# SyncE's transfers of the two down stages of a hybrid decoder layer, chained to each other in program order

## Chip, core and metric

The kernel runs on one core of a Trainium2 chip. The metric is the device time of one execution in microseconds (us); less is better. The core has a matrix engine (PE, with its weight loads as PEld), a vector engine (DVE), a scalar engine (ACT), GpSimd (POOL) and SyncE (SP), which does no arithmetic and issues most of the DMA transfers. Each engine takes its instructions in the order in which the program has them. An instruction whose data are not there holds up all that stand behind it on the same engine, on SP too.

## The reference, cut to what matters

One decoder layer for 2048 tokens and a model width of 1024: three token mixers, an output projection, and a squared-ReLU MLP whose second product is the "down" stage of this case.

```python
    x = x + jnp.einsum("bsc,cd->bsd", mix, w_out)
    h2 = rmsnorm(x, norm2_g)
    ff = jnp.square(jax.nn.relu(jnp.einsum("bsd,df->bsf", h2, w_up)))
    return x + jnp.einsum("bsf,fd->bsd", ff, w_down)   # then a final rmsnorm
```

ff is 2048 x 4096 and w_down 4096 x 1024, all in float32.

## The kernel before

The tokens are worked on in two halves of 1024 (`h` = 0 and 1). For each half come an output projection (`outproj`), an up stage (`up`) and a down stage (`down`); the down stage of half 0 begins at about 968 us of the trace, that of half 1 at 1712 us. Every float32 operand is split by `halves` into a rounded part and a remainder: ACT makes the rounded part (L891), DVE the remainder (L892), and PE multiplies in three passes (L1423 to L1425).

A down stage is a two by two block product in seven products instead of eight (`PRODUCTS` = 1, 2, 7, 6, 4, 5, 3, the order of n = 0 to 6). Each product is eight steps, so a half has 56 steps, g = 0 to 55, of 24 matmuls. One step needs two operands:

- the moving operand, written by the up stage to the DRAM scratch `fscr` and loaded by `s_load` (L1266, 512 KB) into one of six pairs of tiles. `S_AT` names them: in the program's names the pairs are `rounded_73`, `rounded_74`, `rounded_77` twice and `rounded_78` twice, in turn. `s_split` halves it in place. This is what the change's short name calls the first operand of a step;
- the weight block, loaded by `t_load` from w_down: for n = 0 straight into its tile (L1282), later into `kept` (eight blocks, one for each kp = g mod 8) and `second` (a ring of three) (both L1279, 512 KB each). `t_sum` adds or subtracts the two on DVE (L1292, L1294, L1296, result in `kept`), and `t_split` halves the sum into one of six weight pairs. Products 7 and 5 load both blocks for each step, 2 `kept` only, 6, 4 and 3 `second` only.

`ahead(g)` says which of these is asked for at step g: loads up to step g+5, sums up to g+3, splits up to g+2. A pair of the moving operand is free for step g+6 when PE has finished step g. A `kept` block is free when its split is done, a `second` block when its sum is.

The program text is not the order on the engines. A scheduler places each engine's instructions when their operands and tiles are free in its own account; only an explicit dependence added by `tc.add_manual_dep` ties two of them. The output projection already ties its SP instructions in this way (`in_order`); the down stages do not.

At the end of each product (kp = 7) the four PSUM banks are taken out by `evac`: ACT copies for products 1 and 7 (L1429, L1431), DVE additions for product 6 (L1433) and for 2, 4, 5 and 3 (L1436). The first matmul of the next product needs the bank that it writes to be taken out. `res_load` (L1358, 1 MB) and `res_scale` (L1361) bring in the residual. In half 0 the recurrent mixer of half 1 is woven into the down stage by `tick` (L540 to L576, its matmuls L552 to L554); half 1 has nothing woven in.

Of the kernel before, what the change touches and what calls it, by code (L numbers as in the profile page):

```python
# [77 lines left out]
def body(tc, xt, w_in, w_v, w_out, w_up, w_down, vecs, lru_wa, lru_wx, consts, out):  # L78
    nc = tc.nc
# [68 lines left out]
    def conv_bank():  # L148
        return pc.tile([P, NB], F32, name="cb", tag="cb")
# [43 lines left out]
    def v(name, i=0, n=1):  # L193
        at = VEC[name][0] + i
        return vec[:, at:at + n]
# [746 lines left out]
    def out_second(h, pairs):  # L942
        out_load(2, pairs)
        out_load(3, pairs)
        act_load(h, 0, 0, 2)
# [10 lines left out]
    class Weights:  # L956
# [3 lines left out]
        def load(self, f):  # L960
            at = self.at
            nc.sync.dma_start(at[2], w_up[f][:, 2 * NB:3 * NB])
            nc.sync.dma_start(at[0], w_up[f][:, 0:NB])
            nc.sync.dma_start(at[4 + f % 2 * 2], w_up[f][:, NB:2 * NB])
# [25 lines left out]
        def of(self, i, f):  # L990
# [2 lines left out]
            n, c = {1: (0, 0), 6: (0, 1), 7: (2, 0), 5: (2, 1)}.get(i, (4, (i + f + 1) % 2))  # L993
            return [self.pairs[n + j][:, c * NB:(c + 1) * NB] for j in range(2)]

    def outproj(h, wts, banks, begun):
        at, pairs = wts.at, wts.pairs
        s_at = ring(at[0:4])
# [12 lines left out]
        def residual(n):  # L1011
            m, d, tok = where(n)
            nc.sync.dma_start(e_at[n % es], xt[d][:, tok])
# [29 lines left out]

        if not begun:
            out_second(h, pairs)
        queued, mark = [], [len(nc.cur_bb.bb.instructions)]

        def in_order():
            for i in nc.cur_bb.bb.instructions[mark[0]:]:
                if i.engine == mybir.EngineType.SP:  # L1050
                    if queued:
                        tc.add_manual_dep(i, queued[-1].name, mybir.DependencyInfo(
                            mybir.DependencyClass.NoSync, mybir.DependencyReason.DATA), reason="queue")
                    queued.append(i)
            mark[0] = len(nc.cur_bb.bb.instructions)

        residual(0)
        residual(1)
        for n in range(16):
# [274 lines left out]
    def down(h, steps, banks, hooks):  # L1334
# [13 lines left out]
        def part(t, j):  # L1348
            return t[:, j * NB:(j + 1) * NB]

        def tok(m):
            return slice(h * HS + m * NB, h * HS + (m + 1) * NB)
# [21 lines left out]
        def finish(m, zs, load=None):  # L1374
            r, t = sq[m], tmps[0]
            for j in range(3):
                q = tmps[j % 2]
                nc.scalar.activation(q, part(zs[-1], j), AF.Square)
                nc.vector.tensor_add(r, r, q)
                if j == 1:  # L1380
                    yield
            q = tmps[1]
            nc.scalar.activation(q, part(zs[-1], 3), AF.Square)
            nc.scalar.activation(t, mrow[:, m * NB:(m + 1) * NB], AF.Square, scale=RMS_EPS ** 0.5)
            yield
            bank = conv_bank()
            nc.tensor.matmul(bank, ones_d, r, start=True, stop=False)
            nc.tensor.matmul(bank, ones_d, q, start=False, stop=True)
            if load is not None:
                load()  # L1390
            yield
            nc.vector.tensor_add(r, t, bank)
            nc.scalar.activation(r, r, AF.Sqrt)
            yield
            nc.vector.reciprocal(r, r)
            yield
            for dh in (1, 0):
                for j in range(4):
                    d = 4 * dh + j
                    y = part(zs[dh], j)  # L1400
                    nc.vector.scalar_tensor_tensor(y, y, v("final_g", d), r, op0=OP.mult, op1=OP.mult)
                    if j % 2:
                        yield
                        for q in (j - 1, j):
                            (nc.sync if h and not m else nc.gpsimd).dma_start(out[4 * dh + q][:, tok(m)], part(zs[dh], q))
# [32 lines left out]
        def aside_of(n, kp):  # L1438
# [16 lines left out]
            elif i == 5:  # L1455
# [8 lines left out]
                elif kp == 6:  # L1464
                    nc.vector.tensor_add(vv, vv, u)

        for g in range(56):
            n, kp = divmod(g, 8)
            i = PRODUCTS[n]
            ahead(g)  # L1470
            aside_of(n, kp)
            edge = kp in (0, 7)
            if n == 6:
                hooks(kp)
            for x in range(8):
                j, kk = divmod(x, 2) if edge else (x % 4, x // 4)
                matmuls(g, j, kk)
                if kp == 7 and kk:
                    with first():
                        evac(i, j)  # L1480
                if x in (3, 7):
                    tick(DOWN_SHARE)
            if kp == 7:
                if i == 6:
                    nc.vector.tensor_add(vv, vv, u)
                elif i == 2:
                    chores.append(squares(0, z0, True))
                    nc.scalar.dma_start(yscr[:, :, tok(0)].rearrange("j p n -> p j n"), three(z0))
                elif i == 4:
                    chores.append(squares(1, z1, True))  # L1490
                elif i == 5:
                    chores.append(finish(1, (z1, z0)))

        def again():
            nc.gpsimd.dma_start(three(z1), yscr[:, :, tok(0)].rearrange("j p n -> p j n"))
# [134 lines left out]
```

## Time and profile before

| what | value |
|---|---|
| runs | 2038.21, 2041.81 and 2046.28 us; median 2041.81 us |
| profiled execution, its own time | 2037.72 us |
| its span, first to last instruction | 2035.9 us |
| PE busy | 1966.7 us, 97% of the span |
| DVE, ACT, POOL busy | 1466.1, 1053.8 and 168.4 us |
| mean granted clock of PE | 0.994 of full speed |
| DMA | 416.32 MB, mean 204 GB/s |

A group of rows in the profile gives a line, an engine, the tiles (out<-in), a count, busy time, and the idle time before it with what ended that. A row of waits says which instruction waited for which, how long in total, how often, and the longest. Line numbers are those of the kernel before.

### The profile page before, as it was taken

How to read it: one execution, taken by the hardware profiler on the slowest of the kernel's cores; microseconds unless marked ns; L12 is line 12 of the kernel's file. 1: busy time of each engine (PE TensorE's matmuls, PEld its weight loads, DVE VectorE, ACT ScalarE, POOL GpSimd, SP SyncE). 2: the span in 40 equal slices, each digit the busy share in tenths (PEclk: the TensorE clock that was granted, in tenths of full speed). 3: DMA queues.
4: the chain of work that ended last, by engine and by line, in shares of the span. 5: the costliest groups of instructions: out<-in, count | busy, mean ns of one | idle time of the engine just before them, and what ended most of it. 6: DMA issues, size and time to landing. Idle time of an engine off the chain costs nothing.

```text
span 2035.9 us, 25608 instructions
## 1 busy us (share of the span) xinstructions
PE 1966.7 (97%) x8876; PEld 1587.4 (78%) x8876; DVE 1466.1 (72%) x1977; ACT 1053.8 (52%) x1623; POOL 168.4 (8%) x296
## 2 busy tenths in 40 slices
PE   7999999999999999999999899989999999999997
PEld 6877777878777777888788778767888888888885
DVE  7899865578677656878889796677555555686854
ACT  6144875333667655465565654356455455444441
POOL 0123100100113413000000000100000000000001
PEclk9999999999999999999999999999999999999998
DMA  5555584843786647445997765685444437997643
GB/s 166 172 149 161 171 290 152 268 130 114 231 274 189 199 148 254 150 166 189 331 337 244 270 199 166 230 276 180 148 151 151 152 140 253 339 330 234 218 145 114
DMA packets 208766, 416.32 MB, mean 204 GB/s; under 512 B 26134, under 2 KB 34566, under 8 KB 208572
## 3 DMA queue, kind: packets, MB, share of 16 engines
q1 hardware_dynamic: 189220, 358.27, 52.7%
q0 software_dynamic: 16208, 45.91, 7.7%
q10 hardware_dynamic: 3208, 10.49, 1.5%
q8 instruction: 70, 1.15, 0.2%
q14 instruction: 60, 0.49, 0.1%
HBM read 299.79 MB, written 123.19 MB: 208 GB/s over the span
## 4 chain that ended last, share of the span: by engine, by line
PE 73%; DMA 11%; DVE 9%; ACT 4%; issue 3%; SPq 1%; DVEq 0%; POOL 0%; ACTq 0%
PE bank L1113 9%; PE bank L1114 9%; PE bank L1115 9%; PE bank L1423 8%; PE bank L1424 8%; PE bank L1425 8%; PE mm L255 4%; PE mm L258 4%; PE mm L261 3%; DMA rounded<-fscr 2%; DMA pair<-out_w 2%; DMA raw<-in_xt 2%; DVE wide L462 1%; DVE rounded L892 1%; PE bank L929 1%
## 5 line engine op out<-in xcount | busy, mean ns | idle before, releaser
L1113 PE MATMUL bank<-rounded,pair 128*128 128x512 f32 x896 | 354.2, 396 | 2.9 <-ACT low L1193 1.6
L1114 PE MATMUL bank<-rounded,pair 128*128 128x512 f32 x896 | 352.7, 394 | 0.0
L1115 PE MATMUL bank<-rounded,pair 128*128 128x512 f32 x896 | 350.8, 391 | 0.0
L891 ACT CAST rounded<-rounded 128x1024 fp32r<-128x1024 f32 (+1 forms) x168 | 160.4, 967 | 277.5 <-DMA rounded<-fscr 220.7
L892 DVE TENSOR_TENSOR rounded<-rounded 128x1024 fp32r<-128x1024 f32 (+1 forms) x168 | 186.0, 1119 | 124.6 <-ACT rounded L891 124.1
L1423 PE MATMUL bank<-rounded,rounded 128*128 128x512 f32 x576 | 225.4, 391 | 8.4 <-DVE u L1433 5.5
L1425 PE MATMUL bank<-rounded,rounded 128*128 128x512 f32 x576 | 224.7, 390 | 0.0
L1424 PE MATMUL bank<-rounded,rounded 128*128 128x512 f32 x576 | 224.7, 390 | 0.0
L1113 PEld LDWEIGHTS bank<-rounded,pair 128*128 128x128 f32 x896 | 168.1, 188 | 43.5 <-issue 2.6
L1115 PEld LDWEIGHTS bank<-rounded,pair 128*128 128x128 f32 x896 | 168.3, 188 | 37.5 <-issue 0.6
L1114 PEld LDWEIGHTS bank<-rounded,pair 128*128 128x128 f32 x896 | 168.3, 188 | 36.0 <-issue 0.7
L255 PE MATMUL mm<-rounded,rounded 128*128 128x512 f32 x496 | 160.7, 399 | 9.3 <-ACT rounded L235 7.5
L261 PE MATMUL mm<-rounded,rounded 128*128 128x512 f32 x496 | 158.8, 395 | 0.0
L258 PE MATMUL mm<-rounded,rounded 128*128 128x512 f32 x496 | 157.9, 395 | 0.0
L235 ACT CAST rounded<-raw 128x512 fp32r<-128x512 f32 (+1 forms) x96 | 55.8, 583 | 157.3 <-PE mm L258 105.1
L1423 PEld LDWEIGHTS bank<-rounded,rounded 128*128 128x128 f32 x576 | 108.5, 188 | 32.9 <-DVE u L1433 6.1
L891 ACT CAST pair<-wraw 128x1024 fp32r<-128x1024 f32 x64 | 67.2, 1051 | 114.3 <-PE bank L1114 112.7
L1423 PE MATMUL bank<-rounded 128*128 128x512 f32 x320 | 125.5, 392 | 0.7 <-ACT v L1431 0.7
L1424 PEld LDWEIGHTS bank<-rounded,rounded 128*128 128x128 f32 x576 | 108.6, 188 | 22.6
L1425 PEld LDWEIGHTS bank<-rounded,rounded 128*128 128x128 f32 x576 | 108.4, 188 | 22.7
L1425 PE MATMUL bank<-rounded 128*128 128x512 f32 x320 | 124.7, 390 | 1.1 <-DVE rounded L892 1.1
L1424 PE MATMUL bank<-rounded 128*128 128x512 f32 x320 | 124.6, 389 | 0.0
(323 smaller groups left out, 3815.1 us busy)
## 6 DMA issues: line engine op xcount, KB each, us to landing
fscr<-low SPq DMA_DIRECT2D x224, 256.0 KB, 2.2
rounded<-fscr SPq DMA_DIRECT2D x112, 512.0 KB, 4.4
second<-in_w_down SPq DMA_DIRECT2D x80, 512.0 KB, 6.0
kept<-in_w_down SPq DMA_DIRECT2D x48, 512.0 KB, 5.7
raw<-in_w_in SPq DMA_DIRECT2D x64, 256.0 KB, 3.9
wraw<-in_w_up SPq DMA_DIRECT2D x64, 256.0 KB, 2.9
low<-in_w_up SPq DMA_DIRECT2D x64, 256.0 KB, 3.3
pair<-out_w SPq DMA_DIRECT2D x24, 512.0 KB, 5.3
```

Of the source, the lines that this page charges most:

```text
L235: nc.scalar.copy(h, raw)
L255: nc.tensor.matmul(bank, wh[:, sl], ah[:, cols], start=first_, stop=False)
L258: nc.tensor.matmul(bank, wh[:, sl], al[:, cols], start=False, stop=False)
L261: nc.tensor.matmul(bank, wl[:, sl], ah[:, cols], start=False, stop=last_)
L891: nc.scalar.copy(h, raw)
L892: nc.vector.tensor_sub(l, raw, f32(h))
L1113: nc.tensor.matmul(bank, wh[:, sl], hi(x), start=fresh and k == 0, stop=False, **kw)
L1114: nc.tensor.matmul(bank, wh[:, sl], lo(x), start=False, stop=False, **kw)
L1115: nc.tensor.matmul(bank, wl[:, sl], hi(x), start=False, stop=k == KH - 1, **kw)
L1423: nc.tensor.matmul(banks[j], th[:, c], sh[:, x], start=fresh and k0, stop=False, **kw)
L1424: nc.tensor.matmul(banks[j], th[:, c], sl[:, x], start=False, stop=False, **kw)
L1425: nc.tensor.matmul(banks[j], tl[:, c], sh[:, x], start=False, stop=k1, **kw)
```

## The change

The helper that ties SP's instructions to each other in the order in which they were traced moves out of `outproj` into a function of its own, `sp_order`. `outproj` calls it and is as it was. `down` calls it too: once ahead of the 56 steps, and `in_order()` at the end of each step. So every SP instruction traced during a down stage is tied to the one traced before it. The dependence is one of order only: it puts no semaphore on the chip.

```diff
+    def sp_order():
+        queued, mark = [], [len(nc.cur_bb.bb.instructions)]
+
+        def in_order():
+            for i in nc.cur_bb.bb.instructions[mark[0]:]:
+                if i.engine == mybir.EngineType.SP:
+                    if queued:
+                        tc.add_manual_dep(i, queued[-1].name, mybir.DependencyInfo(
+                            mybir.DependencyClass.NoSync, mybir.DependencyReason.DATA), reason="queue")
+                    queued.append(i)
+            mark[0] = len(nc.cur_bb.bb.instructions)
+
+        return in_order
+
     def outproj(h, wts, banks, begun):
...
-        queued, mark = [], [len(nc.cur_bb.bb.instructions)]
-
-        def in_order():
...
+        in_order = sp_order()
         residual(0)
...
+        in_order = sp_order()
         for g in range(56):
             n, kp = divmod(g, 8)
             i = PRODUCTS[n]
...
                 elif i == 5:
                     chores.append(finish(1, (z1, z0)))
+            in_order()
```

The traced order of a step is the one of `ahead`: first the moving operand of step g+5, then the weight block or blocks of step g+5, then a residual load where there is one. PE's and POOL's rows stand in the same order before and after. SP's, DVE's and ACT's change inside the two down stages.

On SP before, in half 0, this stands where products 6 and 4 meet. The two rows of `rounded_78` are the moving operands of steps 34 and 35, the `rounded_73` is that of step 36; `kept_7672` to `kept_7675` are blocks of steps 40 to 43:

```order
L1266 DMA rounded_77<-fscr 128x2x512 x2
L1279 DMA kept_7672<-in_w_down 128x2x512
L1279 DMA kept_7673<-in_w_down 128x2x512
L1266 DMA rounded_78<-fscr 128x2x512
L1279 DMA second_7695<-in_w_down 128x2x512
L1279 DMA kept_7674<-in_w_down 128x2x512
L1266 DMA rounded_78<-fscr 128x2x512
L1279 DMA second_7696<-in_w_down 128x2x512
L1279 DMA kept_7675<-in_w_down 128x2x512
L1279 DMA second_7697<-in_w_down 128x2x512
L1266 DMA rounded_73<-fscr 128x2x512
```

On SP after, the same five moving operands (their line is now L1270, the blocks' L1283), each with the one block of its own step:

```order
L1270 DMA rounded_77<-fscr 128x2x512
L1283 DMA second_7697<-in_w_down 128x2x512
L1270 DMA rounded_77<-fscr 128x2x512
L1283 DMA second_7695<-in_w_down 128x2x512
L1270 DMA rounded_78<-fscr 128x2x512
L1283 DMA second_7696<-in_w_down 128x2x512
L1270 DMA rounded_78<-fscr 128x2x512
L1283 DMA second_7697<-in_w_down 128x2x512
L1270 DMA rounded_73<-fscr 128x2x512
```

The blocks of steps 40 to 43 have moved from between the moving operands of steps 33 to 36 to behind those of steps 40 to 43.

On DVE before, at the end of product 6 of half 0 (steps 30 and 31; L892 is a split, L1292 a sum for product 5, L1433 the evacuation):

```order
L892 TENSOR_TENSOR rounded_78<-rounded_78 128x1024
L892 TENSOR_TENSOR rounded_76<-kept_7675,rounded_76 128x1024
L1292 TENSOR_TENSOR kept_7674<-kept_7674,second_7695 128x1024
L892 TENSOR_TENSOR rounded_78<-rounded_78 128x1024
L892 TENSOR_TENSOR rounded_73<-kept_7676,rounded_73 128x1024
L1292 TENSOR_TENSOR kept_7675<-kept_7675,second_7696 128x1024
L1433 TENSOR_TENSOR u<-u,bank_4017 128x512
L1433 TENSOR_TENSOR u<-u,bank_4018 128x512
```

On DVE after, the same place (L1300 is a sum for product 4, L1437 the evacuation):

```order
L892 TENSOR_TENSOR rounded_78<-rounded_78 128x1024
L1300 TENSOR_TENSOR kept_7674<-second_7696,kept_7674 128x1024
L892 TENSOR_TENSOR rounded_76<-kept_7674,rounded_76 128x1024
L892 TENSOR_TENSOR rounded_78<-rounded_78 128x1024
L1300 TENSOR_TENSOR kept_7675<-second_7697,kept_7675 128x1024
L892 TENSOR_TENSOR rounded_76<-kept_7675,rounded_76 128x1024
L1437 TENSOR_TENSOR u<-u,bank_4017 128x512
L1437 TENSOR_TENSOR u<-u,bank_4018 128x512
```

Before, the evacuation of step 31 stands behind the split of step 36's weights and a sum for step 43. After, it stands behind the sum and the split of step 35's weights. In both, the split of step 35's moving operand stands ahead of it.

## Rows read from the trace of the kernel before

**Rows 1.** The page's busy time, share of the span and instructions of each engine.

```profile
PE 1966.7 (97%) x8876; PEld 1587.4 (78%) x8876; DVE 1466.1 (72%) x1977; ACT 1053.8 (52%) x1623; POOL 168.4 (8%) x296
```

**Rows 2.** PE's waits from 967 to 1304 us: total, times, longest.

```profile
PE bank L1423 <- DVE u L1433: 5.5, 1, 5.5
PE bank L1423 <- DVE z L1436: 1.6, 2, 1.3
PE bank L1423 <- ACT u L1429: 1.3, 1, 1.3
PE bank L1425 <- DVE rounded L892: 1.1, 1, 1.1
PE bank L1423 <- ACT v L1431: 0.7, 1, 0.7
PE cb L276 <- DVE mr L236: 0.7, 1, 0.7
```

**Rows 3.** PE's waits from 1640 us to the end.

```profile
PE cb L1387 <- DVE sum L1379: 1.4, 1, 1.4
```

**Rows 4.** Stretches of half 0: length, PE, PEld, DVE, ACT, POOL, PEclk, DMA share, GB/s.

```profile
1155.70:1161.30 5.60, 0.15 (x1) 0.00 (x0) 4.47 (x6) 5.16 (x6) 0.00 (x0) 0.99 0.92 308
1161.30:1164.70 3.40, 3.38 (x8) 2.71 (x9) 1.76 (x3) 3.14 (x5) 0.00 (x0) 0.52 0.87 313
1164.70:1170.10 5.40, 5.40 (x25) 4.28 (x25) 5.01 (x5) 3.56 (x5) 0.00 (x0) 1.00 0.87 300
```

**Rows 5.** DVE's timeline ahead of the long wait.

```profile
1157.17 1.23 DVE L892 TENSOR_TENSOR rounded<-rounded 128x1024 fp32r<-128x1024 f32 x1 [1.13 <-ACT rounded L891]
1158.31 1.22 DVE L892 TENSOR_TENSOR rounded<-kept,rounded 128x1024 fp32r<-128x1024 f32 x1
1159.45 1.22 DVE L1292 TENSOR_TENSOR kept<-kept,second 128x1024 f32<-128x1024 f32 x1
1160.58 1.28 DVE L1433 TENSOR_TENSOR u<-u,bank 128x512 f32<-128x512 f32 x2
```

**Rows 6.** ACT's timeline there.

```profile
1151.27 1.05 ACT L891 CAST rounded<-rounded 128x1024 fp32r<-128x1024 f32 x1 [11.12 <-DMA rounded<-fscr]
1156.09 1.04 ACT L891 CAST rounded<-rounded 128x1024 fp32r<-128x1024 f32 x1 [2.83 <-DMA rounded<-fscr]
```

**Rows 7.** SP's timeline there (issues only).

```profile
1140.99 1.46 SPq L1279 DMA_DIRECT2D kept<-in_w_down  x2
1142.55 0.63 SPq L1266 DMA_DIRECT2D rounded<-fscr  x1
1143.27 0.77 SPq L1279 DMA_DIRECT2D second<-in_w_down  x1
1149.20 0.37 SPq L1279 DMA_DIRECT2D kept<-in_w_down  x1
1149.66 0.42 SPq L1266 DMA_DIRECT2D rounded<-fscr  x1
```

**Rows 8.** SP's waits from 967 to 1298 us.

```profile
SPq L1266 <- PE bank L1425: 130.2, 35, 7.0
SPq L1279 <- DVE rounded L892: 41.5, 15, 8.1
```

**Rows 9.** SP's timeline in half 1.

```profile
1870.01 0.37 SPq L1266 DMA_DIRECT2D rounded<-fscr  x1
1875.45 0.37 SPq L1266 DMA_DIRECT2D rounded<-fscr  x1
1880.89 0.37 SPq L1266 DMA_DIRECT2D rounded<-fscr  x1
```

**Rows 10.** Landings, min/median/max: all `fscr` operands (L1266), the `second` blocks, the residual loads (L1358).

```profile
DMA to landing us min/median/max: 3.4/4.4/9.2
...
DMA to landing us min/median/max: 3.2/6.0/10.5
...
DMA to landing us min/median/max: 5.1/8.7/9.2
```

**Rows 11.** The second product of half 0 and the fourth of half 1, columns as in rows 4.

```profile
1016.10:1063.10 47.00, 46.71 (x204) 38.21 (x204) 39.75 (x42) 30.92 (x37) 2.14 (x4) 1.00 0.94 333
1842.80:1886.40 43.60, 43.60 (x194) 36.08 (x194) 29.77 (x27) 17.39 (x19) 0.00 (x0) 1.00 0.72 238
```

**Rows 12.** ACT at the end of the first product of half 0.

```profile
1013.62 1.05 ACT L891 CAST rounded<-rounded 128x1024 fp32r<-128x1024 f32 x1 [8.41 <-DMA rounded<-fscr]
1015.52 1.56 ACT L1429 COPY u<-bank 128x512 f32<-128x512 f32 x3
```

More of the change, by code (lines that the diff above doesn't have):

```diff
@@ L1045, in outproj @@
             out_second(h, pairs)
-        queued, mark = [], [len(nc.cur_bb.bb.instructions)]
-        def in_order():
[L1049 to L1055, printed above, removed]
+        in_order = sp_order()
         residual(0)
```

## The prediction

> **What bounds the kernel now.** I read the page's busy times first, then PE's waits by stretch, then, backwards from the longest wait, the timelines of DVE, ACT and SP, and last the landing times. PE is busy for 1966.7 of 2035.9 us [rows 1], so a reordering of transfers can win only what PE loses by waiting inside the two down stages, and can lose anything. In half 0 the waits at the ends of products are 5.5 (product 6, behind the DVE additions of L1433), 1.6 in two (products 2 and 4, L1436), 1.3 (product 1, ACT) and 0.7 us (product 7, ACT): 9.1 us [rows 2]. The other two rows there, 1.1 and 0.7 us, lie in the first steps, where SP's order is not changed. From 1640 us to the end, which holds all of the down stage of half 1, PE waits 1.4 us in all, and that is for the final norm [rows 3]. So half 0 has 9.1 us to give, half 1 nothing.
>
> The long wait has a tail. In the 3.40 us after it PE ran 8 matmuls at a granted clock of 0.52, the lower of its two levels (1.2 GHz), and then 25 in 5.40 us at 1.00 [rows 4]. At the full clock the 8 take 8 x 5.40 / 25 = 1.73 us, so the lower clock cost 3.40 - 1.73 = 1.7 us, behind 5.5 us in which PE had nothing to do. The most that can be won is 9.1 + 1.7 = 10.8 us.
>
> **Where the long wait comes from.** PE stands from 1155.7 to 1161.3 us [rows 4]. The bank that it needs is taken out by the L1433 that begins at 1160.58. DVE was not idle but late: in front stand the split of a moving operand at 1157.17, which had waited for ACT, a weight split and a sum [rows 5]. ACT had waited 2.83 us for the `fscr` transfer that this split reads, and 11.12 us for the one of the step before [rows 6]. That transfer of the step before is step 34's, issued at 1142.55 right behind two `kept` blocks of products to come, and ACT got it only at 1151.27, 8.7 us later, against a median landing of 4.4 [rows 7, 10]. Step 35's was issued at 1149.66, right behind a `kept` block that SP could issue only at 1149.20 [rows 7]; that block is the one of step 42, as the order of before shows, and it waited for a split on DVE to give the block free. So a weight block wanted seven steps later stood in front of an operand that was wanted now. Over this down stage SP waited 41.5 us, in 15 places, for a split to free a block, and 130.2 us, in 35, for PE to free a moving operand [rows 8]. The second kind of wait is the right one: nothing can be loaded sooner. The first is what the chain takes out from in front of it.
>
> **The change, part by part.** (1) No instruction is added or taken out; PE and POOL keep their order; SP issues the same transfers. (2) Moving operands: each now goes out when PE has finished the step that frees its tiles, with nothing ahead of it that waits for anything else. Half 1 shows what this looks like, though its order is the old one: operands leave SP at 1870.01, 1875.45 and 1880.89, one every 5.44 us, which is one step of PE [rows 9], and PE does not wait there [rows 3]. Queued behind such a wait on SP are the blocks of the same step, so they too now go out at the start of a step, five steps before use and not some eleven, as that of step 42 did while PE was in step 31. (3) On DVE the sums for blocks far ahead leave the stretch in front of the evacuations, but the sum and the weight split of step g+4 now stand there, and these need a transfer issued only one step ago.
>
> What (3) may cost must be worked out, end by end. Let T be the start of the last step of product 6, whose end is T + 5.44. Step 35's moving operand is issued at T - 5.44 and its block about 0.4 later (an SP issue took 0.37 to 0.46 [rows 7]). At the median of 6.0 us [rows 10] the block lands at T + 1.0. Then one DVE sum (1.22), ACT's part of the split (1.05), DVE's (1.22) and the first evacuation, half of 1.28 [rows 5, 6], are done at T + 5.1. That is 0.3 us before PE needs the bank. In half 1 the order has an evacuation ahead of that split, so the first bank is free at T + 2.9, 2.5 us early. The same count, with the instructions that stand ahead in the order of after, gives 2.0 us to spare at the end of product 2 (two blocks for each step, a sum, no split) and 1.5 at the end of product 5 (a split, no sum). At the end of product 4 a residual load and its scaling stand ahead; issued two steps before at T - 9.5 and landing in 8.7 us, 9.2 at most [rows 10], it is there at T - 0.3 even then, and 3 us are left. ACT's copies at the ends of products 1 and 7 wait for one moving operand and one split. The one of product 1 waited 8.41 us for an `fscr` transfer [rows 12], with the residual load and POOL's transfers in the queues; the residual load now goes out behind it.
>
> So at median landings every end is met, and all 10.8 us come back; a landing that is late by some microseconds gives back that much at an end, first at the end of product 6 of half 0. The bounds on that are the two ends of the landing row: at 3.2 us nothing is late anywhere; at 10.5, which is 4.5 beyond the median, product 6 of half 0 loses 4.2 and of half 1 2.0, product 2 loses 2.5 and product 5 3.0 in each half, 17.2 us in all. The latest landings belong to stretches like the second product of half 0, where DMA was busy for 0.94 of the time at 333 GB/s [rows 11], because SP had run ahead as far as it could. After, the heaviest steps move three times 512 KB in 5.44 us, 289 GB/s, and most move two, 193 GB/s, about what the 238 GB/s of rows 11 saw in half 1. I therefore take values near the median: 1.2 us left in half 0, where POOL's transfers come between, and 0.5 us new in half 1.
>
> The sum: -9.1 - 1.7 + 1.2 + 0.5 = -9.1 us. On the profiled execution's own time that is 2037.7 - 9.1 = 2028.6 us (a span of some 2026.8). The median of the runs shown stands 4.1 above that execution, so I put the prediction on it: 2041.8 - 9.1 = 2032.7, or 2033 us.
>
> The Trainium skill, "DMA: Bandwidth & Descriptors", section "Anatomy of one DMA", fits a single transfer as about 2.0 us plus its bytes over 436 GB/s (for transfers issued by GpSimd). For 512 KB that estimate is 3.2 us, which is just the minimum here, while the median is 6.0: the transfers of this stage rarely go alone. With the page's figure no end of a product would be late and the sum would be -10.8; by the rows it is -9.1.
>
> **The rivals.** *All of it comes back*: -10.8, with no end late in either half. For it speaks that half 1 has no wait at all [rows 3]; against it the 0.3 us to spare at product 6, with POOL's loads in half 0. From the median of the runs: 2031 us.
>
> *It does not do what it says*: the long wait stays, because in both orders the split of step 35's moving operand stands ahead of the evacuation, and only the small waits change. For it: DVE's order at the end of product 6 has the same number of splits in front. Against it: the transfer that this split waited for was held up by a `kept` block [rows 7], and no such block stands there any more. It gives between -2 and +1, 2040 to 2043 us.
>
> *Slower*: the blocks land too late for the sums that now stand in front of the evacuations. By the spare times above, x us beyond the median cost (x - 0.3) + (x - 2.5) at product 6 of the two halves, 2 (x - 2.0) at product 2 and 2 (x - 1.5) at product 5, together 6x - 9.8; that passes the 10.8 won at x = 3.4, a landing of 9.4 us. At 10.5 it is 17.2 - 10.8 = 6.4 us slower, 2048 us from the median; with the lower clock after four of those waits (1.7 each) 13, or 2055. For it: 9.4 is inside the row's range. Against it: it takes such landings at all ends, with less on the queues than when the row was made. The Trainium skill speaks for it in the same page's "Rules for kernel authors": to overlap DMA with compute, issue the transfer early and wait late. By that rule blocks that are held back to five steps lose cover. The trace agrees only where the queue is not shared with something more urgent.
>
> **How the numbers follow.** Most comes back (-7 to -10): 0.45. All (-10.8): 0.25. Nothing (-2 to +1): 0.20. Slower: 0.10. About 0.5%, 10.2 us, is what a measurement of this kernel can tell from no change. The forecast lies just inside that, so the three runs' own spread of 8 us decides much: I count four fifths of "all" and a quarter of "most" as faster by over 0.5%, 0.20 + 0.11, about 0.32; of "slower" 0.07 beyond 0.5%; the other 0.61 is within. The range reaches from the full gain less the 3.6 us by which the fastest run lies below the median, 2041.8 - 10.8 - 3.6 = 2027.4, to the upper end of "nothing" at 2043: 2027 to 2043, which leaves out the slower case and some spread.
>
> **What would show it.** In the profile after: operands leaving SP every 5.44 us in half 0 too, apart from the woven-in matmuls; SP's waits for a split to free a block gone or down to a few us; no wait of PE over 2 us in either down stage; no stretch at the lower clock near 1160; ACT's long waits for `fscr` in front of the evacuations shorter. The prediction is wrong if PE waits at the ends of products 2, 6 or 5 of half 1 for sums or weight splits that wait for `second` (the slower case), or if the wait at product 6 of half 0 stands with operands issued on time (DVE's order is then the cause, not SP's).

## The result and the profile after

The changed kernel took 2031.96 us in the median (2026.99 to 2037.61, 6 runs) beside 2041.25 us before (2038.21 to 2046.79, 6 runs): a ratio of 0.9948, 95% interval 0.9924 to 0.9971; the medians lie 9.3 us apart. Run a second time beside other kernels it took 2026.68 us, with before at 2038.53 us there (ratio 0.9951, interval 0.9933 to 0.9968).

The profiled execution took 2033.06 us, its span is 2031.3 us. "Stage" means here the time from the start of a down stage's first matmul to the start of its last, read from the trace: 321.9 us in half 0 (before 330.5) and 308.0 us in half 1 (before 306.2). PE's waits after, from 967 to 1304 us, are the answer to [rows 2]:

```profile
PE bank L1427 <- ACT v L1435: 2.8, 1, 2.8
PE bank L1427 <- DVE z L1440: 0.9, 1, 0.9
PE cb L276 <- DVE mr L236: 0.7, 1, 0.7
```

The 5.5 us at the end of product 6 are gone, and so are product 1's 1.3 us. What is left stands at the end of product 7 (ACT, 2.8) and of product 4 (0.9). From 1640 us to the end, beside [rows 3]:

```profile
PE cb L1391 <- DVE sum L1383: 1.4, 1, 1.4
PE bank L1427 <- DVE z L1440: 0.7, 1, 0.7
PE bank L1429 <- DVE rounded L892: 0.5, 1, 0.5
```

SP's waits of after in half 0 (967 to 1298 us), beside [rows 8]:

```profile
SPq L1270 <- PE bank L1429: 222.7, 48, 7.3
...
SPq L1283 <- ACT rounded L891: 1.4, 4, 0.4
...
SPq L1283 <- DVE rounded L892: 0.7, 2, 0.5
```

In the down stage SP now waits for PE and for little else: 0.7 us for the DVE splits that took 41.5. Its timeline at the end of product 6, beside [rows 7], and DVE's there, beside [rows 5]:

```profile
1141.13 0.36 SPq L1270 DMA_DIRECT2D rounded<-fscr  x1
1141.59 0.42 SPq L1283 DMA_DIRECT2D second<-in_w_down  x1
1146.57 0.36 SPq L1270 DMA_DIRECT2D rounded<-fscr  x1
1147.03 0.42 SPq L1283 DMA_DIRECT2D second<-in_w_down  x1
1152.01 0.36 SPq L1270 DMA_DIRECT2D rounded<-fscr  x1
```

```profile
1153.42 1.22 DVE L892 TENSOR_TENSOR rounded<-rounded 128x1024 fp32r<-128x1024 f32 x1
1154.56 1.22 DVE L1300 TENSOR_TENSOR kept<-second,kept 128x1024 f32<-128x1024 f32 x1
1156.89 1.22 DVE L892 TENSOR_TENSOR rounded<-kept,rounded 128x1024 fp32r<-128x1024 f32 x1 [1.12 <-ACT rounded L891]
1158.04 1.28 DVE L1437 TENSOR_TENSOR u<-u,bank 128x512 f32<-128x512 f32 x2
```

Operands leave every 5.44 us. The evacuation begins at 1158.04, its first half is done 0.64 later, at 1158.7, and PE begins the next product at 1158.93 without a wait. The 0.3 us to spare that the prediction had worked out are there, but by luck: step 35's block left SP at 1147.03, 6.4 us ahead of the last step (which began at 1153.45) and not 5.0, because the step between holds matmuls of the mixer, and its sum at 1154.56 waited for the splits ahead of it on DVE and not for the block.

The wait that is left, at the end of product 7, reads like this on ACT and on DVE:

```profile
1110.79 1.04 ACT L891 CAST rounded<-kept 128x1024 fp32r<-128x1024 f32 x1 [1.65 <-DVE kept L1298]
1111.74 1.07 ACT L1435 COPY v<-bank 128x512 f32<-128x512 f32 x2
```

```profile
1105.24 1.28 DVE L570 TENSOR_TENSOR_SCAN m<-m,state 128x512 f32<-128x512 f32 x1
1106.43 0.73 DVE L540 SCALAR_TENSOR_TENSOR m<-m,vec 128x512 f32<-128x512 f32 x1
1107.08 0.15 DVE L572 COPY state<-m 128x1 f32<-128x1 f32 x1
1107.14 0.68 DVE L574 TENSOR_TENSOR m<-m 128x512 f32<-128x512 f32 x1
1107.74 0.75 DVE L540 SCALAR_TENSOR_TENSOR m<-m,vec 128x512 f32<-128x512 f32 x1
1108.40 1.22 DVE L892 TENSOR_TENSOR rounded<-rounded 128x1024 fp32r<-128x1024 f32 x1
1109.54 1.22 DVE L1298 TENSOR_TENSOR kept<-kept,second 128x1024 f32<-128x1024 f32 x1
```

ACT's copy out of the bank stands behind a weight split, that split waits for the sum of step 27, and DVE reaches the sum only at 1109.54, behind five instructions of the woven-in mixer and a split. No transfer is waited for here.

### The profile page after: what moved, and what is told of

It is laid out like the page before. It is cut to its first block, busy times and chain, and to the rows that moved or that the text cites. A ratio compares the mean times of both kernels' runs of the same rounds, so it can differ in the third digit from the quotient of the medians.

```text
span 2031.3 us, 25593 instructions
## 1 busy us (share of the span) xinstructions
PE 1969.5 (97%) x8876; PEld 1589.4 (78%) x8876; DVE 1469.4 (72%) x1977; ACT 1056.9 (52%) x1623; POOL 168.0 (8%) x296
## 4 chain that ended last, share of the span: by engine, by line
PE 77%; DMA 8%; DVE 6%; issue 4%; ACT 4%; SPq 0%; DVEq 0%; POOL 0%; ACTq 0%; POOLq 0%
PE bank L1427 9%; PE bank L1429 9%; PE bank L1428 9%; PE bank L1117 9%; PE bank L1118 9%; PE bank L1119 9%; PE mm L255 4%; PE mm L258 4%; PE mm L261 4%; DMA pair<-out_w 2%; DVE wide L462 1%; PE bank L929 1%; PE bank L927 1%; PE bank L928 1%; PE mm L413 1%
## 5 line engine op out<-in xcount | busy, mean ns | idle before, releaser
L892 DVE TENSOR_TENSOR rounded<-rounded 128x1024 fp32r<-128x1024 f32 (+1 forms) x168 | 186.2, 1119 | 93.0 <-ACT rounded L891 91.4
L891 ACT CAST rounded<-kept 128x1024 fp32r<-128x1024 f32 x80 | 84.0, 1051 | 130.9 <-DVE kept L1296 66.1
L1427 PE MATMUL bank<-rounded 128*128 128x512 f32 x320 | 125.5, 392 | 2.8 <-ACT v L1435 2.8
L892 DVE TENSOR_TENSOR rounded<-kept,rounded 128x1024 fp32r<-128x1024 f32 x80 | 97.7, 1221 | 39.7 <-ACT rounded L891 39.2
```

The lines of the kernel that those rows point to most:

```text
L891: nc.scalar.copy(h, raw)
L892: nc.vector.tensor_sub(l, raw, f32(h))
L1427: nc.tensor.matmul(banks[j], th[:, c], sh[:, x], start=fresh and k0, stop=False, **kw)
```

## The experiments

The first theory was the prediction's: blocks that wait at the head of SP's queue make moving operands late, and the late operands cost PE its time. The rival: what stands on DVE and ACT in front of the evacuations decides, whatever SP does.

The table has, beside the times, two quantities worked out from the traces for the down stage of half 0. "Late" counts the moving operands of steps 6 to 55 that left SP over 1 us after PE began step g-5 (which frees their tiles), and adds up their delays. "Sums ahead" is the mean, over the 32 sums of `t_sum`, of the time from the sum's end on DVE to PE's first matmul of the step that uses it. The ratio is to runs of before on the same chip.

| kernel | median us | ratio, 95% interval | stage 0 | stage 1 | late: count, us | sums ahead us |
|---|---|---|---|---|---|---|
| before | 2041.25 | | 330.5 | 306.2 | 13, 53 | 53.7 |
| after | 2031.96 | 0.9948 (0.9924 to 0.9971) | 321.9 | 308.0 | 1, 5 | 18.5 |
| after_again | 2026.68 | 0.9951 (0.9933 to 0.9968) | 321.6 | 306.3 | 1, 5 | 18.5 |
| e1_half0 | 2025.73 | 0.9927 (0.9910 to 0.9945) | 325.1 | 306.4 | 1, 5 | 18.9 |
| e2_half1 | 2041.59 | 0.9996 (0.9983 to 1.0008) | 332.6 | 307.1 | 14, 54 | 54.5 |
| e3_far_kept | 2022.70 | 0.9911 (0.9893 to 0.9930) | 319.4 | 307.8 | 1, 5 | 18.9 |
| e6_blocks_pool | 2069.67 | 1.0140 (1.0121 to 1.0159) | 347.6 | 326.4 | 1, 5 | 65.3 |
| e7_kept_in_front | 2030.24 | 0.9956 (0.9940 to 0.9973) | 321.8 | 306.4 | 17, 78 | 24.1 |
| e8_late_operand | 2025.80 | 0.9933 (0.9916 to 0.9950) | 317.9 | 306.2 | 3, 16 | 28.0 |
| e9_far_half0 | 2026.27 | 0.9940 (0.9925 to 0.9955) | 319.3 | 308.3 | 1, 5 | 18.8 |
| e14_operand_late | 2024.09 | 0.9917 (0.9898 to 0.9935) | 318.0 | 306.8 | 42, 241 | 22.9 |
| e15_late_in_front | 2029.75 | 0.9939 (0.9922 to 0.9955) | 325.3 | 306.2 | 42, 243 | 23.6 |
| e16_ontime_in_front | 2027.63 | 0.9927 (0.9911 to 0.9943) | 324.7 | 306.2 | 1, 4 | 18.1 |
| e11_evac_first | 2037.36 | 0.9978 (0.9966 to 0.9991) | 328.5 | 307.1 | 11, 23 | 20.6 |

The half 0 of e1_half0 has the order of after on every engine, and e2_half1's that of before (but for one instruction of ACT, one place off). So stage 0 can be read with its scatter between executions: 321.6, 321.9 and 325.1 us for one order, 330.5 and 332.6 for the other.

**Each half alone.** e1_half0 has this edit on the changed kernel, e2_half1 the same with `if h:`.

```diff
-            in_order()
+            if not h:
+                in_order()
```

> The chain in the down stage of half 0 alone. Theory (blocks standing on SP in front of moving operands cost half 0 some 9 us, half 1 had nothing to give): the stage of half 0 takes about 321.9 us as with the full change (before 330.5), the one of half 1 about 306.2 as before, and the whole is 9 to 11 us below before. Rival (the gain depends on both stages, or is spread over the program): the whole is less than 5 us below before, or the stage of half 0 stays above 326.

> The chain in the down stage of half 1 alone. Theory: the stage of half 0 takes about 330.5 us as before with its wait of some 5 us at the end of product 6; the one of half 1 goes from 306.2 to about 308.0 through small waits at the ends of products; the whole is 0 to 2 us above before. Rival (the gain lies in the program as a whole): the whole is some 9 us below before.

The gain comes with half 0's chain. e1_half0's median is 16.1 us below before, where 9 to 11 were expected, and its stage 0 takes 325.1 us and not 321.9. Its profiled execution has a span 11.6 us shorter than before's, of which stage 0 is 5.4; 3.2 lie ahead of it and 3.3 between the two down stages, which the edit does not touch. Chained in half 1 alone, the kernel is at 0.9996 of before, and PE waits in half 0 as before:

```profile
PE bank L1427 <- DVE u L1437: 5.9, 1, 5.9
PE bank L1427 <- DVE z L1440: 2.2, 2, 1.6
PE bank L1427 <- ACT v L1435: 2.1, 1, 2.1
```

**Blocks far ahead on SP.** Two kernels keep the chain but ask for the `kept` blocks of products 7 and 5 early. In e3_far_kept a block is asked for just behind the split that frees it:

```diff
+            while upto["far"] < min(upto["split"] + 8, 56):
+                if upto["far"] // 8 in (2, 5):
+                    t_load(upto["far"], True)
+                upto["far"] += 1
```

In e7_kept_in_front it also stands in front of the operand of seven steps before its own:

```diff
-            for name, to, do in (("s load", 6, s_load), ("s split", 3, s_split), ("sum", 4, t_sum), ("split", 3, t_split), ("load", 6, t_load)):
+            for name, to, do in (("s split", 3, s_split), ("sum", 4, t_sum), ("split", 3, t_split), ("far", 11, far), ("s load", 4, s_load), ("load", 6, t_load)):
```

> The chain stays in both stages, but the kept blocks of products 7 and 5 are asked for some ten steps before use, as early as before the change, and tied in at that place: so they wait on SP for a split on DVE, in front of the next moving operand. DVE's order at the end of product 6 is that of the full change. Theory (head of the queue on SP): SP's waits for splits come back (tens of us), moving operands leave SP up to some 6 us late, and PE waits 2 to 6 us more at the ends of products in half 0; the whole loses 3 to 8 of the 9 us. Rival (DVE's order is the cause): the same as the full change within 2 us, half 0 at about 322.

> The earlier run with far kept blocks asked for them one place behind the split that frees them, and SP hardly waited. Here the chain stays, and each kept block of products 7 and 5 stands in front of the moving operand of the step seven before its own, which is where the block of step 42 stood in front of the operand of step 35 before the change. Theory (an item that waits at the head of SP's queue): SP's waits for splits and sums come back, over 15 us in half 0, operands of product 6 and its likes leave SP some 3 to 6 us after PE has freed their tiles, and PE waits 3 us or more in all at ends of products or in them; half 0 takes 325 us or more, half 1 over 307. Rival (SP's order does not matter as long as it is chained, and DVE's order is the cause): half 0 at 319 to 322.5 as in the other chained kernels.

In e3_far_kept SP's waits did not come back (3.6 us for splits), so it told nothing of them; its stage 0 of 319.4 us is even below the rival's 322. In e7_kept_in_front they did. SP's waits from 974 to 1298 us, and its timeline from the end of product 6 on:

```profile
SPq L1270 <- PE bank L1434: 106.8, 30, 6.2
SPq L1283 <- DVE rounded L892: 67.4, 14, 18.3
```

```profile
1160.74 0.37 SPq L1270 DMA_DIRECT2D rounded<-fscr  x1
1161.15 0.62 SPq L1283 DMA_DIRECT2D second<-in_w_down  x1
1180.40 0.37 SPq L1283 DMA_DIRECT2D kept<-in_w_down  x1
1180.87 0.41 SPq L1270 DMA_DIRECT2D rounded<-fscr  x1
```

For 19 us SP issues nothing, because a `kept` block at its head waits for a split; the operand behind it, of step 38, leaves 13.7 us late, 15.0 us ahead of its step. Such waits are longer than before the change (67.4 us against 41.5 [rows 8]), and stage 0 still takes 321.8 us, with 0.7 us of wait at the end of product 6. The 325 us or more that the theory expected did not come, nor the 307 in half 1 (306.4). This kernel tests SP's waits alone: its sums are done 24.1 us before use and not 53.7, so the far sums of before are not back on DVE.

**The control with the operand asked for as late.** e8_late_operand is e7_kept_in_front without the far blocks.

```diff
-            for name, to, do in (("s load", 6, s_load), ("s split", 3, s_split), ("sum", 4, t_sum), ("split", 3, t_split), ("load", 6, t_load)):
+            for name, to, do in (("s split", 3, s_split), ("sum", 4, t_sum), ("split", 3, t_split), ("s load", 4, s_load), ("load", 6, t_load)):
```

> Control of the kernel with the kept blocks in front: the chain with the moving operand asked for as late as there (step g+3, behind sum and split), but with the kept blocks back beside the second blocks of their own step, so that nothing on SP waits for a split seven steps ahead. Theory (an item that waits at the head of SP's queue): half 0 at 319 to 323, SP's waits for splits under 5 us, the whole within 3 us of the change. Rival (late asking for the operand is what costs): as slow as the kernel with the kept blocks in front.

It has the shortest stage 0 of all, 317.9 us, with two waits of PE, both in the first steps:

```profile
PE bank L1429 <- DVE rounded L892: 0.8, 1, 0.8
PE cb L276 <- DVE mr L236: 0.7, 1, 0.7
```

So neither asking late nor SP's waits bring the loss back by themselves, and the first theory fell. The new one: a late transfer costs only where an instruction that waits for it stands in front of an evacuation.

**Lateness by itself, and with a tie.** e14_operand_late makes each operand of half 0 from step 16 on wait for one more step of PE. To do so it also changes the order of `ahead` in both halves: the weight block of step g+5 is asked for first, then the operand of step g+4. e15_late_in_front has the same and also ties the first evacuation of products 2, 6, 4, 5 and 3 of half 0 behind the split of the operand four steps ahead; e16_ontime_in_front has the tie with operands on time. Both ask for an operand's split two steps earlier than after does. So the three differ from after in more than the one thing each is meant to test. In these three the last product of each half multiplies with other weight blocks (mostly those of three steps later), of the same number and size; the first six products have their own.

```diff
         def s_load(g):
...
+            if g >= 16 and not h:
+                tc.add_manual_dep(nc.cur_bb.bb.instructions[-1], stepped[g - 5], mybir.DependencyInfo(
+                    mybir.DependencyClass.Sync, mybir.DependencyReason.DATA), reason="late")
...
-            for name, to, do in (("s load", 6, s_load), ("s split", 3, s_split), ("sum", 4, t_sum), ("split", 3, t_split), ("load", 6, t_load)):
+            for name, to, do in (("load", 6, t_load), ("s load", 5, s_load), ("s split", 3, s_split), ("sum", 4, t_sum), ("split", 3, t_split)):
```

`stepped[g]` is the last matmul of step g. In the two others `s split` has 5 for its 3; e16_ontime_in_front has no `late` dependence and asks for the operand of step g+5 ahead of its block, as after does. The tie stands behind `evac(i, j)`, `stepped["split"]` being the last split of an operand that is traced by then:

```diff
+                    if not h and j == 0 and i not in (1, 7):
+                        tc.add_manual_dep(nc.cur_bb.bb.instructions[-1], stepped["split"], mybir.DependencyInfo(
+                            mybir.DependencyClass.NoSync, mybir.DependencyReason.DATA), reason="behind")
```

> The change, with every moving operand of half 0 from step 16 on held back by one step more (it waits for PE to finish step g-5 and not g-6), 5.44 us late each, some 40 times over 200 us of lateness against 53 before the change. The order of the arithmetic engines is left to follow. New theory (lateness on SP costs only where an instruction that waits for the late operand stands in front of an evacuation): half 0 at 317 to 322.5, since the order follows. Old theory (operands that leave SP late cost PE's time): half 0 at 326 or more.

> The same lateness, and the evacuation of the first bank at the ends of products 2, 6, 4 and 5 of half 0 is tied behind the split of the moving operand four steps ahead, on DVE. New theory: the operand leaves SP at the start of the product's last step, lands 4.4 us later, its split takes 1.05 on ACT and 1.22 on DVE, so the bank is free some 2 us after PE wants it at the median landing and 7 at the slowest: waits of 2 to 7 us at up to four ends, half 0 at 326 or more. Rival (order does not matter): as the kernel with the lateness alone, within 2 us.

> The same tie of the evacuations behind the split four steps ahead, but with the operands on time. New theory: it takes both, so there is no wait of more than 1 us at the ends of products 2, 6, 4 and 5, and half 0 is at 317 to 323. Rival (a split in front of an evacuation costs by itself): waits as in the kernel with both, half 0 at 326 or more.

With 42 operands late by 241 us in all, e14_operand_late has a stage 0 of 318.0 us and no wait at the end of any product. DVE at the end of product 6 shows why (L1305 a sum, L1442 the evacuation):

```profile
1147.13 1.22 DVE L1305 TENSOR_TENSOR kept<-second,kept 128x1024 f32<-128x1024 f32 x1
1148.32 0.69 DVE L1442 TENSOR_TENSOR u<-u,bank 128x512 f32<-128x512 f32 x1
1149.69 0.69 DVE L1442 TENSOR_TENSOR u<-u,bank 128x512 f32<-128x512 f32 x1 [0.68 <-PE bank L1434]
...
1152.27 1.28 DVE L1442 TENSOR_TENSOR u<-u,bank 128x512 f32<-128x512 f32 x2
1153.46 1.22 DVE L892 TENSOR_TENSOR rounded<-rounded 128x1024 fp32r<-128x1024 f32 x1
```

The split of step 35's operand (1153.46) now stands behind the evacuation, and the first bank is out at 1149.0, 3.2 us before PE begins the next product at 1152.2. The two kernels with the tie did not settle the rest. Their waits in half 0, first e15_late_in_front, then e16_ontime_in_front:

```profile
PE bank L1433 <- DVE z L1446: 3.1, 5, 1.8
...
PE bank L1433 <- DVE u L1443: 0.4, 1, 0.4
```

```profile
PE cb L552 <- ACT mr L235: 1.9, 1, 1.9
PE bank L1433 <- DVE z L1446: 1.6, 2, 1.2
...
PE cb L553 <- DVE mr L236: 0.8, 1, 0.8
```

Waits behind additions are 3.5 us with both and 1.6 with the tie alone, so the expected 2 to 7 us at up to four ends were too much. None of the four forecasts for the stage came true: e15_late_in_front took 325.3 us and not 326 or more, but 7 more than with the lateness alone (a stretch at the lower clock in its first steps, at 972 us, among them); e16_ontime_in_front took 324.7 us, above the 323 of the new theory, with a wait of 1.2 us at the end of product 4, and below the rival's 326. Both stages lie at the upper end of the scatter of the change itself (321.6 to 325.1), so the ends of products do not decide whether it takes both. The 1.9 and 0.8 us of e16_ontime_in_front say something else. ACT's split of step 23's operand, four steps ahead, waited 6.31 us for a transfer that had left SP on time at 1069.93 and took 10.3 us to land, and the mixer's cast behind it (1082.26) came late for PE. So the place of the split matters for the mixer too, and an operand that leaves on time can still land late.

**The other repairs.** e6_blocks_pool is the kernel before with the weight blocks issued by POOL:

```diff
-                nc.sync.dma_start(two(dst), w_down[rows, :, b * NB:(b + 1) * NB].rearrange("k p n -> p k n"))
+                nc.gpsimd.dma_start(two(dst), w_down[rows, :, b * NB:(b + 1) * NB].rearrange("k p n -> p k n"))
```

e11_evac_first is the kernel before with what `ahead` traces in the next product tied behind the evacuation, on the engine that takes the bank out (`out_of` holds the last evacuation by engine):

```diff
+            behind = len(nc.cur_bb.bb.instructions)
             ahead(g)
+            for i_ in nc.cur_bb.bb.instructions[behind:]:
+                if i_.engine in out_of:
+                    tc.add_manual_dep(i_, out_of[i_.engine], mybir.DependencyInfo(
+                        mybir.DependencyClass.NoSync, mybir.DependencyReason.DATA), reason="evac")
```

> The kernel before, without the chain, with the weight blocks of the down stages issued by POOL and only the moving operands left on SP. DVE's order at the end of product 6 is that of before: the split of step 36's weights and a far sum stand ahead of the evacuation. Theory (head of the queue on SP): the moving operands leave SP every 5.44 us, ACT's waits for them shrink, and the 5.5 us wait at the end of product 6 of half 0 is under 1 us, down stage of half 0 some 7 to 9 us shorter than before, unless POOL's own woven-in work holds the blocks up. Rival (DVE's order is the cause): operands on time, and the wait of about 5 us stays.

> The kernel before, without the chain on SP. At each end of a product the splits and sums that later steps ask for are tied behind the evacuation, on the engine that takes the banks out. New theory (what stands in front of an evacuation decides): the wait of 5.5 us at the end of product 6 of half 0 is under 1 us, half 0 at 317 to 323, the whole 7 to 13 us below before, although operands still leave SP late in places. Old theory (SP's order decides): if operands are late by tens of us in all as before, half 0 stays at 327 or more.

e6_blocks_pool is 1.4% slower: the blocks now wait at the head of POOL's queue (52.0 us in half 0 for splits on DVE alone), and PE waits some 20 us in half 0 and 14 in half 1. Its longest wait, 6.2 us at 992 us, is for a cast of the mixer that stood on ACT behind an operand's split, which had waited 5.86 us for its transfer. Operands leave SP on time, as the rival had it, and 4.2 us of the wait at the end of product 6 stay (PE's waits from 1160 to 1180 us, and DVE there):

```profile
PE bank L1423 <- DVE u L1433: 4.2, 1, 4.2
```

```profile
1168.35 1.22 DVE L892 TENSOR_TENSOR rounded<-kept,rounded 128x1024 fp32r<-128x1024 f32 x1
1172.48 1.23 DVE L1292 TENSOR_TENSOR kept<-kept,second 128x1024 f32<-128x1024 f32 x1 [2.91 <-DMA kept<-in_w_down]
1173.62 1.28 DVE L1433 TENSOR_TENSOR u<-u,bank 128x512 f32<-128x512 f32 x2
```

A sum for a later product stands in front of the evacuation and waits 2.91 us for its block. With operands issued on time, a late block holds up the evacuation. DVE's order in this kernel is not that of before all over (its sums are done 65.3 us ahead), so it is no clean test of the rest.

e11_evac_first loses the 5.5 us at once and gives most of it back:

```profile
PE cb L552 <- ACT mr L235: 3.4, 2, 2.0
PE cb L553 <- DVE mr L236: 2.2, 1, 2.2
PE bank L1423 <- DVE z L1436: 1.4, 2, 1.1
```

5.6 us are now waits of the woven-in mixer's matmuls. Ahead of one of them, at 1084.5 us, ACT's cast for the mixer stood behind a split that had waited 3.09 us for PE to free its tile. Stage 0 is 328.5 us, the whole 0.9978 of before. So the wait at the end of product 6 went, as the new theory said, with SP's order untied and 11 operands still late, but the stage missed that theory's 317 to 323 us and lies where the old one had put it (327 or more), with its waits in other places.

**The change once more, and a sum of two.** e9_far_half0 is e3_far_kept with the chain in half 0 alone.

> The changed kernel once more, beside the others. Expected: ratio to before 0.995, 2029 to 2034 us. The profile of its first run had 4.3 us more ahead of the down stage of half 0 than before, in stages that the change does not touch, with four spells of the lower clock there. If that belongs to the build, it stands here again (the down stage of half 0 begins at 971 us or later); if it is chance of the single execution, it begins at 965 to 968.

> The kept blocks of products 7 and 5 asked for behind the split that frees them, and the chain in half 0 alone. If the 2.5 us that the far blocks won in half 0 and the 1.6 us that half 1 wins without the chain add up: down stages of 319.4 and 306.3 us, and 2020 to 2024 us in all. Rival (the far blocks' gain in the medians is scatter): no faster than the chain in half 0 alone, 2025 to 2029 us.

```diff
+            while upto["far"] < min(upto["split"] + 8, 56):
...
-            in_order()
+            if not h:
+                in_order()
```

The 4.3 us ahead of half 0 did not stand in the second execution: the stage began at 967.5 us, not 972.1, and the median of 2026.68 us is below the 2029 expected. And the gains of e3_far_kept and e1_half0 did not add up: 2026.27 us. Every kernel with the chain in half 0 is faster than before; between e3_far_kept, e14_operand_late, e1_half0 and e8_late_operand, at ratios of 0.9911 to 0.9933 with intervals of some 0.0018 to either side, nothing is told apart.

## Why the prediction was right, and which steps were not

**The sum.** Forecast -9.1 us, measured -9.3 in the median of the first comparison. That the two agree to 0.2 us is luck: the medians of the second comparison lie 11.9 us apart and the two profiled executions of before and after 4.7. In half 0 the forecast was -9.1 - 1.7 + 1.2 = -9.6; the stage shrank by 8.6 and 8.9 us in the two executions of after and by 5.4 in e1_half0. In half 1 it was +0.5; measured +1.8 and +0.1. For the first execution the terms are: waits at ends 9.1 before, 3.8 after (2.8, 0.9 and one of 0.1), so 5.3 won; the 1.7 us of the lower clock behind the long wait; 1.1 of a wait in the first steps, which the prediction had left out and which is not there in these two executions; together 8.1 of the 8.6.

**The term "1.2 us left in half 0" was too small**: 3.8, 3.6 and 4.0 us stood at the ends of products in the three executions with this order. The step that failed first is "ACT's copies at the ends of products 1 and 7 wait for one moving operand and one split". At product 7 ACT's split also waits for a sum on DVE, which the mixer's instructions hold up. The count of spare time at an end went through transfers, splits and evacuations, and not through what else is on the engine. "No wait of PE over 2 us" failed with it. At product 4, where the count had 3 us left, PE waited 0.9 us in half 0 and 0.7 in half 1 of the first execution: the scaling of the residual did not wait for its load in either. In half 0 (1202.31, 2.28 us) it stood on DVE behind three instructions of the mixer, a sum and a split; in half 1 an addition of 2.29 us stood between it and the evacuation. One reading was off as well, though the sum does not use it: the slowest landing of the blocks in [rows 10], 10.5 us, was of one issued at 1800.0, in half 1, and not in the busy stretch of half 0.

**The step "Where the long wait comes from" was half right.** The chain on SP is as the rows had it, and all that was said of SP came: waits for splits gone, operands every 5.44 us, no lower clock near 1160; ACT's waits for `fscr` in half 0 are down from 89.7 to 50.5 us. But the inference that an operand that leaves SP late is what costs PE its time fell. With 241 us of lateness (e14_operand_late) or 78 us (e7_kept_in_front), stage 0 takes 318.0 and 321.8 us, as good as with operands on time. An operand has time: from step 6 on even those of before left SP 23.9 us or more ahead of the step that uses them, and a landing of 4.4 us in the median [rows 10] and 2.3 of splitting are small beside that. What it lacked in before was a place on DVE behind the evacuation: its split, wanted four steps later, stood in front of an addition wanted at once, together with a weight split wanted five steps later and a sum wanted at step 43, 65 us later [rows 5].

The trace of before also says how little of the long wait the operands can be. On DVE ahead of [rows 5] stand the sums of steps 40, 41 and 42, and the first two wait for their own blocks:

```profile
1146.81 1.22 DVE L1292 TENSOR_TENSOR kept<-kept,second 128x1024 f32<-128x1024 f32 x1 [2.48 <-DMA kept<-in_w_down]
1149.97 1.23 DVE L1292 TENSOR_TENSOR kept<-kept,second 128x1024 f32<-128x1024 f32 x1 [0.80 <-DMA kept<-in_w_down]
...
1154.82 1.22 DVE L1292 TENSOR_TENSOR kept<-kept,second 128x1024 f32<-128x1024 f32 x1
```

The block of step 42, issued at 1149.20 [rows 7], landed at 1154.69, so its sum could not begin before 1154.8 however early the operands came. Behind it stand two splits and the sum of step 43, 1.14 us apart, so the evacuation could have begun at about 1159.4 and not at 1160.58. As an estimate from these rows, with DVE's order and the blocks' times as they were, operands on time would have won 1.2 of the 5.5 us; the rest lies with the far sums in front of the evacuation and the waits for their blocks. The 4.2 us left in e6_blocks_pool agree with that. The prediction had laid the wait to the operands; of the sums' own waits for blocks it says nothing.

**What the chain changed for PE** is therefore to be looked for on DVE and ACT. With the chain a sum can stand no further ahead than its block, and the blocks go out five steps ahead: sums are done 18.5 us before use in the mean, not 53.7. That is part (3) of the prediction, which was counted only as a cost. In every kernel with the chain in half 0 the wait at the end of product 6 is under 1 us; in both executions with the old order it is 5.5 and 5.9, and with the old SP order but the evacuations tied in front (e11_evac_first) there is none. The rival "it does not do what it says" had named DVE's order as the cause; it was wrong in that the wait went away, because the chain changed that order too.

**"Slower"** did not come: no kernel with its blocks held back to five steps is slower than before as a whole, and the largest loss in a stage is 1.8 us in half 1, not seen again in the second execution. The Trainium skill, "DMA: Bandwidth & Descriptors", "Rules for kernel authors", to issue a DMA early and wait late, had spoken for this rival; no run here bears it out. In kernels whose sums are 23 to 28 us ahead (e14_operand_late, e8_late_operand) the wait at product 7 is gone, but it is at most 0.7 us too in three others with sums at 18 to 19 us (e3_far_kept, e9_far_half0, e16_ontime_in_front). Nor does a row show the limit that the prediction put on the rule, a queue that is not shared: in half 1 of before SP's queue is shared in the same way, and PE does not wait [rows 3].

**Open.** The split of the long wait into 1.2 us and the rest is an estimate: no kernel had before's order on DVE with all transfers on time. e6_blocks_pool came nearest, and there the blocks were late. In half 1, sums 53.5 us ahead cost nothing (no wait in [rows 3]); that it takes the woven-in mixer beside them is likely, but no run shows it. And the stages do not account for the whole times: e1_half0's two down stages are 5.2 us shorter than before's, its median 16.1. Each kernel has one profiled execution, and before's 2037.72 us is below all six runs of the first comparison; what the rest of the gain is stays open.

## What to carry to other kernels

A wait at the head of an in-order DMA queue is not yet a loss: first compare how far ahead of its use the delayed transfer goes out, then look at which engine has an instruction that depends on it in front of something urgent. Ordering one queue reorders the engines behind it, since the scheduler places work when its operands can be there; read what stands in front of the evacuations, not only the transfers. Loading much further ahead than needed can cost time by drawing later work in front of what is wanted now, as at the end of product 6.

## What was not expected of the hardware

One program spends different time in stages that no edit touches, in good part because the lower clock falls in different places. The stretch from 353.8 to 360.7 us in the first execution of after and in the second (columns as in rows 4):

```profile
353.80:360.70 6.90, 5.82 (x18) 5.53 (x19) 3.04 (x4) 2.23 (x4) 2.10 (x4) 0.52 0.65 178
```

```profile
353.80:360.70 6.90, 6.76 (x38) 6.31 (x38) 3.43 (x5) 2.66 (x5) 2.09 (x4) 1.00 0.70 197
```

At 0.52 (1.2 GHz) PE ran 18 matmuls, at 1.00 (2.4 GHz) 38. Likewise a wait of 3.1 us at product 7 is followed by a granted clock of 0.61 for 4.2 us in e1_half0, and one of 3.2 us in the second execution of after by 1.00. The waits at the ends of products agree better between executions of one order than the whole times do (3.8, 3.6 and 4.0 us in all for the new order, 9.1 and 10.4 for the old), so the stages and their waits say more of a cause here than single times.
